# The 72 stores of the merge's tanh gates: issued from ScalarE's queue instead of SP's

## The chip, the cores and the metric

One core of one Trainium2 chip runs the kernel. The metric is the device time of one execution in microseconds (us), the median of several; lower is better. The core has five engines that run their own instruction queues in order: TensorE (PE, matmuls and transposes into PSUM), VectorE (DVE), ScalarE (ACT), GpSimd (POOL), and SP, which computes nothing and here issues all transfers between SBUF and DRAM.

## The reference, cut to what matters

Two layers of a mixer over 512 latent tokens and 256 context tokens, width 1024, all in float32. Each layer makes from `h @ w_in` the inputs of three attention branches (neighbourhood, latent, differential), twelve gate paths `z`, and three merge gates `gm` of 1024 channels each, 24 blocks of 128 channels. Only the end of a layer matters here:

```
y = (sigmoid(g_na)   * ((o_na   * silu(z_na))   @ w_br[0])
   + sigmoid(g_mla)  * ((o_mla  * silu(z_mla))  @ w_br[1])
   + sigmoid(g_diff) * ((o_diff * silu(z_diff)) @ w_br[2]))
x = x + gate * (y @ w_out)
```

The sigmoid is computed as (tanh(g/2) + 1) / 2. The tanh is what is stored and read again later.

## The kernel before, in words

A layer (`mixer`) has two parts. In the first, twelve steps each project the operands of one attention pair (`proj_nd`, `proj_m`), one gate path (`zgate`) and some of the 24 merge-gate blocks (`gm`), while the attention of the pair of the step before runs (`attn`). `NGM` says how many gate blocks fall to which step, `ADA` which steps also take a part of the modulation vector (`ada_half`). In the second part, `branch` multiplies the attention outputs with `w_br` and merges them with the stored gates, and `out_proj` does the last projection.

Every float32 matmul is three matmuls (`mm3`, lines 115 to 117) of operands that are split into a high and a low part. A weight block comes by DMA into one of seven raw buffers (`ws`, line 138), ScalarE makes the high part (`w`, line 122), VectorE or GpSimd the low part (line 127), in one of nine buffers each.

`gm` (line 1001 and after) takes one block of 128 gate channels: 24 matmuls for each range of tokens into the one PSUM bank `fl`, then ScalarE's tanh from `fl` into the one SBUF buffer `th` (line 1011), then a DMA of `th` to the DRAM tensor `thd` (line 1012). Layer 0 has two ranges of 384 tokens for a block, layer 1 one range of 512, so there are 24 x 2 + 24 = 72 tanhs and 72 stores, of 192 and 256 KB. `zgate`, `ada_half` and some of the second part use the same bank `fl`. In the second part line 987 reads the gates back, one load for each block and branch.

The order of each engine's queue is fixed when the kernel is built. A planner simulates the engines on a model of their costs; at each point it takes, of the instructions that could start, the one with the earliest due time. The due times are set with `at`: a base for the step, an offset for the kind of work (`PRI`) and some hand-set shifts (`SHIFT`). The planner also places the waits between engines. Other DMAs that the text speaks of: line 232 loads `aw`, the weights of `ada_half`, into two buffers for the matmuls of line 237; line 598 loads `ct` for the latent attention; line 974 loads `uraw`, the attention outputs. ScalarE's other work in the same stretches: the exponentials of the softmax (line 717), the copies of transposed probabilities out of PSUM (line 705), and the high parts of lines 122 and 522.

Of the kernel before, what the change touches and what calls it, by code (L numbers as in the profile page):

```python
# [52 lines left out]
class Mixer:  # L53
# [948 lines left out]
    def gm(self, l, i, pool):  # L1002
        nc = self.nc
        ws = self.units(self.io["w_gm"][l, i])
        for c0, w in self.cols(l):
            c = slice(c0, c0 + w)
            ps = self.fl()
            for k in range(KT):
                self.mm3(ps[:, :w], ws[k], [self.h[j][:, k, c] for j in range(2)], k == 0, k == KT - 1)
            th = pool.tile([P, 512], F32, tag="th", name=self.n("th"))[:, :w]  # L1010
            nc.scalar.activation(th, ps[:, :w], AF.Tanh, scale=0.5)
            nc.sync.dma_start(self.th[i][:, c], th)

    def diff_tables(self, l, pool):
        nc = self.nc
# [174 lines left out]
```

## Time and profile before

| | |
|---|---|
| median of 3 runs | 1928.85 us (1923.16 to 1929.49) |
| the profiled execution | 1923.38 us |
| its span, first to last instruction | 1921.6 us |
| PE busy | 1857.9 us, 97% of the span |
| VectorE busy | 1192.0 us, 62% |
| ScalarE busy | 938.8 us, 49% |
| GpSimd busy | 762.1 us, 40% |
| DMA | 1 queue for the program's data, 41.1% of 16 engines' span |

In the rows, PE is TensorE's matmuls, PEld its weight loads, and a name with q (SPq, ACTq) is an engine's sequencer, which waits and issues while the engine itself is idle. "A <- B" in a list of waits says that A stood idle until B ended. L1012 is line 1012 of the kernel.

### The profile page before, as it was taken

What the parts mean: (1) busy time and instruction counts of PE and PEld (TensorE: products, weight loads), DVE (VectorE), ACT (ScalarE), POOL (GpSimd) and SP (SyncE); (2) the same over time, 40 slices, a digit from 0 to 9 for tenths busy, and PEclk for the clock granted to TensorE, in tenths of its full rate; (3) what the DMA queues carried; (4) which work ended last, traced back from release to release, by engine and by line L of the source; (5) the groups of instructions that cost most, each with busy time, mean ns of one, the idle gap of its engine ahead of it and who ended that gap; (6) DMA issues with size and microseconds to landing.
All of it is one profiled execution on the core that took longest, in us unless ns stands there. A gap on an engine that the chain in (4) does not pass through costs nothing.

```text
span 1921.6 us, 33888 instructions
## 1 busy us (share of the span) xinstructions
PE 1857.9 (97%) x11707; PEld 1725.0 (90%) x11707; DVE 1192.0 (62%) x2698; ACT 938.8 (49%) x2422; POOL 762.1 (40%) x1057
## 2 busy tenths in 40 slices
PE   7999999999999999999999999999899999999998
PEld 3999999999899998999999988898799798889878
DVE  4556567646865655557663455668668665766763
ACT  4445455445644544546432344556456455555531
POOL 3343333233433333243355454444334343443363
PEclk8999999999999999999999999999999999999999
DMA  9454223343545334324655234423522523442663
GB/s 314 159 178 142 64 67 100 102 132 86 159 136 169 85 120 134 103 89 120 228 161 171 99 122 132 122 75 91 167 64 71 161 78 92 123 131 60 192 194 117
DMA packets 184824, 245.38 MB, mean 128 GB/s; under 512 B 22454, under 2 KB 148040, under 8 KB 184652
## 3 DMA queue, kind: packets, MB, share of 16 engines
q1 hardware_dynamic: 184652, 243.21, 41.1%
q8 instruction: 93, 1.52, 0.3%
q14 instruction: 79, 0.65, 0.1%
HBM read 190.45 MB, written 46.53 MB: 123 GB/s over the span
## 4 chain that ended last, share of the span: by engine, by line
PE 87%; DVE 4%; DMA 3%; ACT 2%; POOL 2%; issue 1%; SPq 0%; ACTq 0%; DVEq 0%; POOLq 0%
PE pj L115 11%; PE pj L117 11%; PE pj L116 11%; PE fl L115 10%; PE fl L116 10%; PE fl L117 9%; PE sc L712 6%; PE bk L867 4%; PE bk L702 4%; PE bk L833 2%; PE sc L754 1%; PE pj L662 1%; DMA aw<-in_w_ada 1%; PE pj L473 1%; PE fl L237 1%
## 5 line engine op out<-in xcount | busy, mean ns | idle before, releaser
L122 ACT CAST w<-ws 128x384 fp32r<-128x384 f32 (+3 forms) x520 | 237.4, 473 | 256.2 <-PE fl L116 153.0
L127 POOL TENSOR_TENSOR w<-ws,w 128x384 fp32r<-128x384 f32 (+3 forms) x260 | 242.5, 938 | 298.3 <-ACT w L122 275.3
L115 PE MATMUL fl<-h,w 128*128 128x384 f32 (+1 forms) x864 | 314.4, 364 | 6.4 <-DVE zs L414 4.7
L115 PE MATMUL pj<-w,h 128*128 128x384 f32 (+2 forms) x944 | 313.6, 335 | 2.0 <-DVE kl L127 1.1
L117 PE MATMUL fl<-h,w 128*128 128x384 f32 (+1 forms) x864 | 310.7, 360 | 2.2 <-DVE w L127 1.3
L116 PE MATMUL pj<-w,h 128*128 128x384 f32 (+2 forms) x944 | 309.8, 329 | 1.0 <-POOL w L127 1.0
L116 PE MATMUL fl<-h,w 128*128 128x384 f32 (+1 forms) x864 | 310.0, 359 | 0.0
L117 PE MATMUL pj<-w,h 128*128 128x384 f32 (+2 forms) x944 | 309.2, 331 | 0.7 <-POOL h L127 0.6
L127 DVE TENSOR_TENSOR w<-ws,w 128x384 fp32r<-128x384 f32 (+2 forms) x260 | 170.6, 659 | 72.4 <-ACT w L122 67.2
L167 POOL TENSOR_TENSOR ss<-ss,nhalf 128x4 f32<-128x4 f32 (+1 forms) x144 | 143.1, 994 | 177.8 <-DVE ss L166 161.7
L717 ACT ACTIVATE P<-sc,st 128x768 f32<-128x768 f32 (+1 forms) x192 | 159.5, 832 | 100.8 <-DVE st L798 43.0
L764 POOL TENSOR_SCALAR P<-P,st 128x512 f32<-128x512 f32 (+1 forms) x128 | 107.9, 845 | 241.1 <-DVE st L760 211.4
L115 PEld LDWEIGHTS pj<-w,h 128*128 128x128 f32 x944 | 178.5, 190 | 8.9 <-issue 3.0
L117 PEld LDWEIGHTS pj<-w,h 128*128 128x128 f32 x944 | 177.7, 189 | 5.7 <-DVE h L368 3.3
L115 PEld LDWEIGHTS fl<-h,w 128*128 128x128 f32 x864 | 163.1, 189 | 20.2 <-DVE zs L414 6.5
L116 PEld LDWEIGHTS pj<-w,h 128*128 128x128 f32 x944 | 179.1, 190 | 1.7 <-POOL w L127 1.3
L706 DVE TENSOR_TENSOR pt<-bk,pt 128x512 fp32r<-128x512 f32 (+1 forms) x256 | 147.5, 585 | 52.1 <-ACT pt L705 49.6
L117 PEld LDWEIGHTS fl<-h,w 128*128 128x128 f32 x864 | 162.9, 189 | 14.0 <-POOL w L127 1.6
L116 PEld LDWEIGHTS fl<-h,w 128*128 128x128 f32 x864 | 163.1, 189 | 9.5
L705 ACT CAST pt<-bk 128x512 fp32r<-128x512 f32 (+1 forms) x256 | 127.2, 507 | 77.0 <-PE bk L702 73.9
L712 PE MATMUL sc<-qk,qk 96*128 96x512 f32 (+3 forms) x592 | 144.3, 337 | 1.4 <-ACT P L717 1.0
L702 PE MATMUL bk<-cst,P 128*128 128x128 f32 x832 | 128.9, 273 | 5.0 <-DVE ss L166 2.0
(239 smaller groups left out, 3915.5 us busy)
## 6 DMA issues: line engine op xcount, KB each, us to landing
ws<-in_w_qkv SPq DMA_DIRECT2D x128, 192.0 KB
ws<-in_w_gm SPq DMA_DIRECT2D x96, 192.0 KB
aw<-in_w_ada SPq DMA_DIRECT2D x32, 512.0 KB
ct<-cqd SPq DMA_DIRECT2D x40, 384.0 KB
ct<-ckd SPq DMA_DIRECT2D x48, 256.0 KB
ws<-in_w_z SPq DMA_DIRECT2D x48, 192.0 KB
thd<-th SPq DMA_DIRECT2D x48, 192.0 KB
ws<-in_w_br SPq DMA_DIRECT2D x48, 192.0 KB
```

Source lines behind the costliest of these rows:

```text
L115: mm(out, a[0], b[0], start=first, stop=False)
L116: mm(out, a[0], b[1], start=False, stop=False)
L117: mm(out, a[1], b[0], start=False, stop=last)
L122: nc.scalar.copy(hi, src)
L127: (nc.gpsimd if le == "g" else nc.vector).tensor_tensor(lo, src, f(hi), ALU.subtract)
L167: nc.gpsimd.tensor_tensor(out, out, self.nhalf[:, :cols], ALU.pow)
L702: nc.tensor.transpose(pt[:, i * P:(i + 1) * P], src[:, (b0 + i) * P:(b0 + i + 1) * P], self.ident)
L705: nc.scalar.copy(h, v)
L706: nc.vector.tensor_tensor(lo, v, f(h), ALU.subtract)
L712: mm(s[:, d0:d0 + w], x, y, start=i == 0, stop=i == len(ops) - 1)
L717: nc.scalar.activation(p, src, AF.Exp, bias=st[:, m:m + 1], accum_out=st[:, o:o + 1])
L764: nc.gpsimd.tensor_scalar(p, p, st[:, 4 + m:5 + m], 0.0, ALU.mult, ALU.add)
```

## The change

The DMA of line 1012 is issued from ScalarE's queue. It moves the same bytes between the same places, and it still has to follow the tanh of line 1011. All other DMAs stay on SP's queue.

```diff
             th = pool.tile([P, 512], F32, tag="th", name=self.n("th"))[:, :w]
             nc.scalar.activation(th, ps[:, :w], AF.Tanh, scale=0.5)
-            nc.sync.dma_start(self.th[i][:, c], th)
+            nc.scalar.dma_start(self.th[i][:, c], th)
```

## Rows read from the trace of the kernel before

**Rows 1.** The page, busy time and share of the span and instructions, by engine.

```profile
PE 1857.9 (97%) x11707; PEld 1725.0 (90%) x11707; DVE 1192.0 (62%) x2698; ACT 938.8 (49%) x2422; POOL 762.1 (40%) x1057
```

**Rows 2.** Busy time by engine in the two stretches that hold the stores.

```profile
core 0: us, PE busy (x) PEld busy (x) DVE busy (x) ACT busy (x) POOL busy (x), PEclk, DMA share, GB/s
142.00:918.00 776.00, 762.78 (x5068) 732.50 (x5068) 487.29 (x1132) 402.10 (x1059) 266.31 (x382) 1.00 0.38 115
1196.00:1786.00 590.00, 573.04 (x3613) 517.41 (x3612) 397.36 (x929) 322.50 (x828) 242.35 (x347) 0.99 0.35 105
```

**Rows 3.** Waits of PE, whole span: us in total, times, longest.

```profile
PE fl L237 <- DMA aw<-in_w_ada: 6.2, 4, 3.1
...
PE bk L702 <- DVE pt L706: 1.4, 3, 0.8
...
PE fl L115 <- ACT th L1011: 1.2, 4, 0.4
...
PE sc L712 <- ACT P L717: 1.0, 2, 0.8
```

**Rows 4.** The page, chain that ended last, shares by engine.

```profile
PE 87%; DVE 4%; DMA 3%; ACT 2%; POOL 2%; issue 1%; SPq 0%; ACTq 0%; DVEq 0%; POOLq 0%
```

**Rows 5.** Instructions of the store's line and the tanh's line: ns min/median/max.

```profile
L1012 SPq DMA_DIRECT2D thd<-th x72: 319/327/1151, 142.6 to 1785.2; - x72
L1012 SPq EVENT_SEMAPHORE  x70: 17/17/17, 141.2 to 1785.1; - x70
...
L1011 ACT ACTIVATE th<-fl x72: 479/492/619, 142.1 to 1782.7; 128x384 f32<-128x384 f32 x48, 128x512 f32<-128x512 f32 x24
```

**Rows 6.** Waits of SP's queue: us in total, times, longest.

```profile
SPq L138 <- POOL w L127: 270.2, 150, 10.2
...
SPq L1012 <- ACT th L1011: 88.1, 41, 6.9
...
SPq L1012 <- ACT qk L122: 15.0, 7, 7.4
...
SPq L1012 <- ACT qk L130: 6.9, 2, 4.4
...
SPq L1012 <- ACT pt L705: 2.9, 6, 1.3
```

**Rows 7.** ScalarE in time around three tanhs: start us, us, instruction [idle before].

```profile
171.71 0.51 ACT L1011 ACTIVATE th<-fl 128x384 f32<-128x384 f32 x1
172.10 0.39 ACT L705 CAST pt<-bk 128x256 fp32r<-128x256 f32 x1
...
912.67 0.48 ACT L1011 ACTIVATE th<-fl 128x384 f32<-128x384 f32 x1
913.18 0.36 ACT L870 COPY ot<-bk 64x256 f32<-64x256 f32 x1
...
1782.68 0.59 ACT L1011 ACTIVATE th<-fl 128x512 f32<-128x512 f32 x1
1783.17 0.36 ACT L705 CAST pt<-bk 128x256 fp32r<-128x256 f32 x1
```

**Rows 8.** SP's issue of the store at 171.71, start us, us.

```profile
172.25 0.32 SPq L1012 DMA_DIRECT2D thd<-th  x1
```

**Rows 9.** ScalarE's longest wait by cause: us in total, times, longest.

```profile
ACT w L122 <- PE fl L116: 153.0, 152, 4.8
```

**Rows 10.** SP's issues in time before two late loads: start us, us, issue.

```profile
1365.90 0.33 SPq L1012 DMA_DIRECT2D thd<-th  x1
...
1368.02 0.33 SPq L598 DMA_DIRECT2D ct<-ckd  x1
1368.62 0.93 SPq L232 DMA_DIRECT2D aw<-in_w_ada  x2
...
1488.39 0.38 SPq L1012 DMA_DIRECT2D thd<-th  x1
1489.33 0.33 SPq L138 DMA_DIRECT2D ws<-in_w_gm  x1
1489.75 0.41 SPq L598 DMA_DIRECT2D ct<-ckd  x1
1490.25 0.93 SPq L232 DMA_DIRECT2D aw<-in_w_ada  x2
```

## The prediction

> **What bounds the kernel now.** I read the page first: PE is busy 1857.9 of 1921.6 us, 97% [rows 1]. Whatever moves the time has to add to PE's idle time, 63.7 us in all, or take from it. The busy time by stretch says how much of that lies where the stores are: 776.00 - 762.78 = 13.2 us from 142 to 918 us and 590.00 - 573.04 = 17.0 us from 1196 to 1786 us, together 30.2 us [rows 2]. That is the most that any rearrangement there could give back. The list of PE's waits then shows what this idle time is made of: many small waits, the largest group 6.2 us for the loads of `aw`, and almost none for ScalarE: 1.2 us for the tanh itself, 1.0 us for the exponentials [rows 3]. The chain of work that ended last agrees: PE 87%, DMA 3%, ACT 2%, and SP's own issuing 0% [rows 4].
>
> The store itself is next. On SP one issue takes 319 to 1151 ns, 327 in the median [rows 5]. SP often stands before it: 88.1 + 15.0 + 6.9 + 2.9 = 112.9 us in 41 + 7 + 2 + 6 = 56 waits ended by ScalarE [rows 6]. The reader should see that SP is early, not late: it waits for the tanh and issues at once, as at 172.25 us, 0.03 us after the tanh that began at 171.71 and took 0.51 [rows 7, 8].
>
> **Part 1: what SP is rid of.** 72 issues x 0.327 us = 23.5 us of issuing and the 112.9 us of standing. What stood behind a store can go earlier, in the longest case by 7.4 us [rows 6]. Most of that is weight loads, and they are not short: SP waits 270.2 us for their buffers to come free from GpSimd alone [rows 6], and ScalarE's high parts wait 153.0 us for PE to give buffers back [rows 9]. Loads that come earlier only fill raw buffers earlier. That is worth nothing as long as the seven raw buffers stay ahead; if that cover is gone, each late block is a PE wait on line 115 to 117, which now hardly occurs.
>
> The exception is `aw`, the only load for which PE loses time. Before the largest of its waits a store is issued at 1365.90, but a load of `ct` comes between, at 1368.02, and `aw` goes at 1368.62, 2.4 us after the store was done [rows 10]: it was not the store that held it. At 1488.39 a store took 0.38 us and two more loads followed it before `aw` at 1490.25 [rows 10]; without it `aw` goes about 0.4 us earlier. Bounds of the gain: 0 and the whole 6.2 us; I take 0.4, by the second place, where the store's own slot is all that `aw` gets back.
>
> The Trainium skill, "DMA: Bandwidth & Descriptors", section "Issuing engines are not separate DMA queues", says that issuing from several engines only saves the sequencer's time to start a transfer. By it SP's standing would count for nothing and the sum would gain at most the store's slot; by the list of SP's waits, read alone, a gain up to the 6.2 us would be open. The order of issues before the late loads sides with the page at both places.
>
> **Part 2: what ScalarE takes on.** The trace has no DMA issued by ScalarE, so the price comes from SP's rows. The issue must wait until the tanh is written (0.03 us on SP), then takes 0.327 us, and the next instruction can no longer start before the tanh has ended, as it does now at 172.10 against an end at 172.22, some 0.1 us [rows 7]. That is 0.46 us where ScalarE has work ready. It has in 27 of the 72 cases, the first at 171.71 and the last at 1782.68 [rows 7]: 27 x 0.46 = 12.4 us. In 17 more the gap is under 0.36 us, like the 0.03 us behind the tanh of 912.67 [rows 7], and 0.18 us is lost on average: 3.1 us. In the other 28 the idle time covers the issue. Sum: 15.5 us of delay on an engine that is idle 373.9 + 267.5 = 641 us in these stretches [rows 2]. Bounds: 0, if the order is such that no store meets ready work, and 72 x (0.03 + 1.151 + 0.1) = 92 us if each issue took SP's longest.
>
> How much reaches the end? ScalarE's share of the chain is 2% for 49% busy [rows 1, 4], so one us in 25 of its time counts: 15.5 / 25 = 0.6 us. The cover is the slack of PE behind ScalarE: VectorE's low parts come between, and PE waits for those of line 706 1.4 us in all [rows 3]. As one late copy also delays VectorE's instruction behind it, I double this to 1.3 us. What is late next, should the cover go, is the copy of line 705, then the low part of line 706 and PE's product with the values.
>
> Each store has besides a wait of its own ahead of it, which never lasted on SP: 17 ns, 70 times [rows 5]. What it is for the row doesn't say. I cost it at nothing; if it lasted on ScalarE, the exponentials would queue behind it.
>
> **Part 3: nothing from the buffer.** `th` has one buffer, but the store is already issued 0.03 us after most tanhs, so it can't come free sooner, and the transfer is the same.
>
> **Part 4: the order.** The planner builds all queues anew with the store on ScalarE, and may place other instructions elsewhere. No row prices that. Bounds: it gives back the 30.2 us of idle time in these stretches [rows 2], or adds as much. With no reason for a sign I take 0 and keep a part of both ends for the range.
>
> **Sum.** 1.3 - 0.4 = about +1 us: 1924.4 us against the profiled 1923.38 (span 1921.6 and 1.8 around it). The median of the runs, 1928.85, lies 5.5 us above that execution, so the forecast for a median is 1930 us. Differences under 0.3%, 5.8 us, can't be told from no change here.
>
> **Rivals.**
> Slower by ScalarE's queue: the store stops the softmax. Place: copies of line 705 and exponentials of line 717 right behind a store. Price: the 15.5 us in full, or 72 x 0.46 = 33 us if the new order sets each store ahead of ready work: 1944 to 1962 us. It decides when PE's slack behind ScalarE is under 0.46 us, or where the store's second wait lasts. For it: 27 back-to-back places. Against it: PE waits so little for ScalarE now [rows 3], and 641 us of idle time. Chance 0.2.
>
> Faster by SP's queue: freed loads end the 6.2 us of `aw` waits and some of the small ones: about 1921 us. For it: 112.9 us of standing. Against it: the order before those loads [rows 10], and this only just passes 0.3%. Chance 0.05.
>
> A new order that matters more than either: up to some 15 us both ways, half of the 30.2: 1914 to 1944 us. For it: PE's idle time is many waits of single places [rows 3], which any shift of the queues exchanges for others. Against it: the work per engine is the same. Chance 0.35: 0.2 faster, 0.15 slower by over 0.3%.
>
> The change doing nothing that can be seen is part of the forecast.
>
> **How the numbers follow.** Forecast, the order much as it is and both prices hidden: 0.40, its own range 1923 to 1934.6 us. Faster 0.2 + 0.05 = 0.25, slower 0.2 + 0.15 = 0.35. The range runs from 1914, the lower end of a new order, to 1950, inside ScalarE's rival; some 0.1 lies above and 0.05 below.
>
> **What would show it.** Right: no wait of SP on line 1012; 72 issues of some 0.33 us on ScalarE's queue with idle time of that size behind 40 or so tanhs; PE's busy time within 1 us of 1857.9 and its idle time within 5 us of 63.7; waits of PE for ScalarE of a few us. Wrong: waits of PE for lines 705, 706 or 717 of 10 us and more (ScalarE's rival); the `aw` waits gone and the time down (SP's rival); PE's waits at quite other places with as much work done (a new order). An issue on ScalarE far from 0.33 us would make part 2 wrong even if the time is right.

## The result, and the profile after

The changed kernel takes 1946.34 us (median of 4 runs, 1944.1 to 1948.49) against 1926.01 us for the kernel before (4 runs). The ratio is 1.0107, 95% interval 1.0078 to 1.0135: slower by some 20 us. The profiled execution took 1947.38 us, with a span of 1945.2 us, 23.6 us more than the span of before.

The page of the changed kernel, busy time by engine, which answers to [rows 1]:

```profile
PE 1868.8 (96%) x11707; PEld 1734.5 (89%) x11707; DVE 1199.0 (62%) x2698; ACT 938.2 (48%) x2422; POOL 766.7 (39%) x1057
```

The same instructions ran on every engine, and ScalarE's busy time is the old one to 0.6 us. PE shows where the time is, in two halves: its idle time went from 63.7 to 1945.2 - 1868.8 = 76.4 us, 12.7 us more, and its busy time, for the same 11707 matmuls, from 1857.9 to 1868.8 us, 10.9 us more. Together that is the 23.6 us. The split holds for this pair of executions: TensorE's mean granted clock (1 is full speed) differs between executions of one kernel, from 0.989 to 0.996 among 23 of the kernel before, which took 1928.9 and 1916.63 us at those two ends.

The store itself is what the change says. The instructions of line 1012 in the changed kernel (ns min/median/max, first and last start), which answer to [rows 5]:

```profile
L1012 ACTq DMA_DIRECT2D thd<-th x72: 325/326/365, 144.3 to 1805.8; - x72
L1012 ACTq EVENT_SEMAPHORE  x58: 17/17/17, 143.8 to 1733.4; - x58
```

72 issues of 0.326 us on ScalarE's queue, none over 0.365 us, and each wait that stands as an instruction of its own lasts 17 ns. The last store starts at 1805.8 us, where it started at 1785.2 before [rows 5]: 20.6 of the 23.6 us are lost by the time that the last gate is made. ScalarE in time at one of these stores, in the changed kernel:

```profile
173.18 0.51 ACT L1011 ACTIVATE th<-fl 128x384 f32<-128x384 f32 x1
173.56 0.39 ACT L705 CAST pt<-bk 128x256 fp32r<-128x256 f32 x1
173.72 0.33 ACTq L1012 DMA_DIRECT2D thd<-th  x1
174.09 0.28 ACT L632 ACTIVATE qn<-pj 128x128 f32<-128x128 f32 x1
```

The tanh ends at 173.69. Here the planner set a copy between tanh and store, and the issue runs from 173.72 to 174.05 while that copy still works until 173.95. In 33 of the 72 cases one to three other instructions stand between the two; in the other 39 the store follows its tanh directly.

The waits of PE in the changed kernel (total, times, longest), which answer to [rows 3]:

```profile
PE pj L473 <- DVE qn L467: 11.3, 8, 4.2
PE fl L237 <- DMA aw<-in_w_ada: 11.2, 4, 5.6
...
PE bk L845 <- POOL s L842: 2.7, 1, 2.7
...
PE sc L712 <- DMA qk<-qk: 2.0, 1, 2.0
```

The same list of the kernel before, for two lines that [rows 3] don't have:

```profile
PE pj L350 <- DVE ssx L166: 9.4, 1, 9.4
PE pj L473 <- DVE qn L467: 6.3, 5, 2.8
```

None of the changed kernel's four is a wait for ScalarE. (PE's longest single wait, over 9 us on line 350, stands at the start of both kernels and has no part in the difference.) The waits for VectorE's `qn` grew from 6.3 to 11.3 us and those for `aw` from 6.2 to 11.2 us, though SP now issues these loads with no store ahead of them. SP in time before the longest wait for `aw`, in the changed kernel, which answers to the first half of [rows 10]:

```profile
1376.39 0.33 SPq L598 DMA_DIRECT2D ct<-cqd  x1
1377.13 0.33 SPq L598 DMA_DIRECT2D ct<-ckd  x1
1377.73 0.93 SPq L232 DMA_DIRECT2D aw<-in_w_ada  x2
```

PE's product with them, before (the wait that [rows 10] lead up to) and after (start, duration, idle time before):

```profile
1375.48 1.08 PE L237 MATMUL fl<-aw,sT 128*32 128x256 f32 x8 [3.07 <-DMA aw<-in_w_ada]
```

```profile
1384.57 1.08 PE L237 MATMUL fl<-aw,sT 128*32 128x256 f32 x8 [5.58 <-DMA aw<-in_w_ada]
```

From issue to product it is 1375.48 - 1368.62 = 6.86 us before and 1384.57 - 1377.73 = 6.84 us after: the load is as fast as it was. But PE had other work for 6.86 - 3.07 = 3.8 us of that before, and for 6.84 - 5.58 = 1.3 us now. The order leaves it less to do in between.

The other half, PE's busy time, is seen in stretches around a wait. Busy time (instructions) of PE, PEld, DVE, ACT and POOL, then granted clock, DMA share and GB/s, in the changed kernel:

```profile
304.00:312.50 8.50, 8.50 (x64) 8.43 (x63) 7.83 (x21) 5.49 (x16) 6.82 (x7) 1.00 0.36 104
312.50:317.20 4.70, 0.51 (x5) 0.27 (x3) 4.51 (x10) 3.26 (x8) 2.25 (x4) 0.94 0.48 153
317.20:323.50 6.30, 6.10 (x21) 5.71 (x22) 4.19 (x11) 2.75 (x7) 1.36 (x2) 0.50 0.14 31
323.50:330.00 6.50, 6.50 (x54) 6.47 (x52) 3.71 (x7) 2.48 (x6) 0.00 (x0) 1.00 0.40 115
```

PE is busy throughout, then for 0.51 of 4.70 us, and behind that the granted clock is 0.50, the lower of its two levels (1.2 instead of 2.4 GHz): 6.10 us of work hold 21 matmuls, where the next 6.50 us hold 54 (not all of the same shape). The mean granted clock tells how much of this there is. Span and clock of the core before, and after:

```profile
core 0: 1921.6 us, clock 0.993
```

```profile
core 0: 1945.2 us, clock 0.984
```

With half the time lost at the lower level, that is from 0.007 x 1921.6 / 0.5 = 27 us (the start of the program included) to 0.016 x 1945.2 / 0.5 = 62 us, some 35 us more. One us of work at half clock is half a us too long, so 35 us explain up to 17 of PE's longer busy time; 10.9 were measured. Counted by the trace's clock records instead, PE worked 25.2 us at half clock before and 53.2 us after; half of the difference is 14.0 us. The seven stretches at half clock that lie in the two parts with the stores, in the changed kernel, each follow or overlap a PE wait of 1.6 to 5.6 us; but behind a wait of 2.8 us at 735.1 us in the kernel before the clock stayed at 1.00, so not every wait brings one.

### The profile page after: what moved, and what is told of

It reads as the page before. It is cut to its first block, busy times and chain, and to the rows that moved or that the text cites. A ratio compares the mean times of both kernels' runs of the same rounds, so it can differ in the third digit from the quotient of the medians.

```text
span 1945.2 us, 33846 instructions
## 1 busy us (share of the span) xinstructions
PE 1868.8 (96%) x11707; PEld 1734.5 (89%) x11707; DVE 1199.0 (62%) x2698; ACT 938.2 (48%) x2422; POOL 766.7 (39%) x1057
## 4 chain that ended last, share of the span: by engine, by line
PE 86%; DVE 5%; DMA 3%; ACT 2%; POOL 2%; issue 2%; SPq 0%; DVEq 0%; ACTq 0%; POOLq 0%
PE pj L115 11%; PE pj L117 11%; PE pj L116 11%; PE fl L115 10%; PE fl L116 10%; PE fl L117 10%; PE sc L712 6%; PE bk L867 4%; PE bk L702 4%; PE bk L833 2%; PE sc L754 1%; DMA aw<-in_w_ada 1%; PE pj L662 1%; PE pj L473 1%; PE fl L237 1%
## 5 line engine op out<-in xcount | busy, mean ns | idle before, releaser
L127 DVE TENSOR_TENSOR w<-ws,w 128x384 fp32r<-128x384 f32 (+2 forms) x260 | 175.5, 678 | 81.8 <-ACT w L122 74.5
```

Of the source, the lines that this page charges most:

```text
L127: (nc.gpsimd if le == "g" else nc.vector).tensor_tensor(lo, src, f(hi), ALU.subtract)
```

## The experiments

An engine's queue can be held to a given order with edges between neighbours that add no semaphore:

```diff
+        for a, b in zip(q, q[1:]):
+            tc.add_manual_dep(ins[b], ins[a].name, dep, reason="pin")
```

So the two things that the change does, another engine that issues and another order of the queues, can be taken apart. Between the kernels before and after, 4892 lines of PE's program stand elsewhere; in the traces, at least 1424 of the 11707 matmuls have to be moved to make one order of PE into the other.

**The order of before, stores on ScalarE.** All queues keep the order of before; the store stands right behind its tanh. The trace has the 11707 matmuls in the order of before, and ScalarE's instructions too.

```diff
-            nc.sync.dma_start(self.th[i][:, c], th)
+            nc.scalar.dma_start(self.th[i][:, c], th)
...
+            pin(nc, tc)
```

> All queues keep the order of the kernel before, instruction by instruction; only the 72 stores leave SP's queue and stand in ScalarE's right behind their tanh. So this holds the price of the issue on ScalarE and nothing of a new order. If the new order costs the 20 us (my theory): a ratio to the kernel before of 0.997 to 1.003, about 1926 us. If ScalarE's queue costs it (the rival): at least half of the loss, a ratio of 1.005 to 1.012, and more than in the changed kernel where 33 of its 72 stores stand two to four instructions behind the tanh, since here each stands directly behind it.

Measured: 1924.01 us (12 runs) against 1922.73 (23 runs), ratio 1.0003 (0.9988 to 1.0017). Its page, its stores and two of its waits of PE, and the first line of SP's waits:

```profile
PE 1859.7 (97%) x11707; PEld 1726.8 (90%) x11707; DVE 1194.8 (62%) x2698; ACT 939.4 (49%) x2422; POOL 761.7 (40%) x1057
```

```profile
L1012 ACTq DMA_DIRECT2D thd<-th x72: 325/326/365, 142.7 to 1786.4; - x72
```

```profile
...
PE fl L237 <- DMA aw<-in_w_ada: 7.9, 4, 3.0
PE pj L473 <- DVE qn L467: 6.3, 5, 2.8
```

```profile
SPq L138 <- POOL w L127: 306.6, 160, 10.5
```

ScalarE at the first of the places where it has work ready behind the tanh, which answers to [rows 7]:

```profile
171.67 0.51 ACT L1011 ACTIVATE th<-fl 128x384 f32<-128x384 f32 x1
172.22 0.33 ACTq L1012 DMA_DIRECT2D thd<-th  x1
172.58 0.37 ACT L705 CAST pt<-bk 128x256 fp32r<-128x256 f32 x1 [0.40 <-ACT th L1011]
```

The copy of line 705 now starts 0.40 us after the tanh has ended, where it started 0.12 us before that [rows 7]. Compared tanh by tanh between the two traces, the next instruction starts later by 18.8 us in all: 13.4 us in the 27 cases with work ready, 5.4 us in the 17 with a small gap, nothing in the other 28. So ScalarE is held up, but it costs PE nothing: PE's idle time is 1923.7 - 1859.7 = 64.0 us, against 63.7. Nor does SP's relief give anything: its wait for raw buffers rose from 270.2 us [rows 6] to 306.6, and the waits for `aw` did not shrink (7.9 against 6.2 us).

**The order of after, stores on SP.** The other half alone: the same edges, now with the changed kernel's order.

```diff
             nc.sync.dma_start(self.th[i][:, c], th)
...
+            pin(nc, tc)
```

> All queues have the order of the changed kernel, but the 72 stores are issued by SP, each at its place in the planner's overall order. So this holds the new order and no issue on ScalarE. If the new order costs the 20 us (my theory): a ratio to the kernel before of 1.008 to 1.013, about 1945 us. If ScalarE's queue costs it: 0.997 to 1.004.

Measured: 1942.47 us (5 runs), ratio 1.0103 (1.0078 to 1.0127), the loss of the changed kernel within its interval. Its waits of PE:

```profile
PE pj L473 <- DVE qn L467: 12.0, 8, 4.2
...
PE fl L237 <- DMA aw<-in_w_ada: 8.1, 2, 5.5
...
PE sc L712 <- DMA qk<-qk: 3.2, 1, 3.2
PE bk L845 <- POOL s L842: 2.7, 1, 2.7
```

These are the waits of the changed kernel, with no store on ScalarE's queue. Its page (the span is 1939.6 us, the mean granted clock 0.988):

```profile
PE 1863.3 (96%) x11707; PEld 1731.2 (89%) x11707; DVE 1200.1 (62%) x2698; ACT 937.4 (48%) x2422; POOL 765.9 (39%) x1057
```

PE's idle time is 1939.6 - 1863.3 = 76.3 us, that of the changed kernel (76.4). Its busy time is 5.4 us over that of before in this execution, at a higher clock than the 0.984 of the changed kernel's. The loss is the order.

**Another order with the stores on SP.** Is it any order but the one of before?

```diff
-    PRI = dict(step=2200, attn=500, prep=1000, pm=1500, ...
+    PRI = dict(step=2200, attn=500, prep=1000, pm=1520, ...
```

> The stores are SP's as before; one offset of a due time is 1520 instead of 1500 (the latent projection), which changes 1367 lines of PE's order against 4892 in the changed kernel. If any order other than the one of the kernel before is slower (theory: the due times are fitted to that one order): a ratio of 1.002 to 1.010. If orders drawn by chance scatter around the old one: 0.995 to 1.005 with either sign. If ScalarE's queue is all that matters: 0.998 to 1.002.

Measured: 1929.11 us (12 runs), 1.0033 (1.0018 to 1.0048), with 1367 of PE's lines elsewhere. Another order costs, but a third of the 1.07%.

**The longest waits filled.** The changed kernel's order, with PE's waiting matmuls set behind the work that follows them at seven of its long waits (4.2 us at 317.22, 5.6 at 1384.57, and five of 1.4 to 3.1). In PE's order, at the first of them (this is a list of instructions, not code):

```diff
 L702 bk<-cst,P
-L473 pj<-cst,qn   (waited 4.21 us)
 L702 bk<-cst,P
 L115 fl<-h,w
 ...
+L473 pj<-cst,qn
```

> The order of the changed kernel, stores on ScalarE, but at seven places where PE stood 1.4 to 5.6 us there (19.8 us in all: lines 473, 237, 473, 473, 712, 237, 237) the waiting matmuls are put behind the PE work that followed them, as much of it as the wait was long. If the loss sits in these waits and in the half clock behind them (my theory): at least half of the 20 us comes back, a ratio to the kernel before of 1.000 to 1.006. If the new order costs by many small shifts everywhere (the rival): less than a quarter comes back, 1.008 to 1.011.

Measured: 1950.39 us (4 runs) against 1922.72 (7 runs), 1.015 (1.013 to 1.017). Nothing came back, and neither forecast held. But the seven fills did not take PE's idle time away. The page (the span is 1952.8 us):

```profile
PE 1872.6 (96%) x11707; PEld 1740.2 (89%) x11707; DVE 1200.1 (61%) x2698; ACT 937.6 (48%) x2422; POOL 767.4 (39%) x1057
```

PE is idle for 1952.8 - 1872.6 = 80.2 us, against 76.4 in the changed kernel. The waits for `qn` of line 467 and for `aw` fell from 22.5 to 9.0 us together, and others came in their place. PE in time at the first of the seven, in this kernel:

```profile
310.86 0.60 PE L702 MATMUL bk<-cst,P 128*128 128x128 f32 x4
316.53 1.12 PE L702 MATMUL bk<-cst,P 128*128 128x128 f32 x4 [5.07 <-POOL P L764]
...
319.36 0.52 PE L115 MATMUL fl<-h,w 128*128 128x384 f32 x1
...
322.00 0.34 PE L116 MATMUL fl<-h,w 128*128 128x384 f32 x1
```

The matmul of line 473 is out of the way, and the next one in the queue waits 5.07 us for GpSimd in its place. Behind it a matmul of the same shape takes 0.52 us, and 2.6 us later 0.34: the granted clock is 0.50 from 316.50 to 320.80 us and 1.00 behind that. So filling one place moved the wait to another; whether the loss would go if the waits themselves went is not shown by this run.

**Four issues for one store, order of before.** How much does ScalarE's cover hold?

```diff
-            nc.scalar.dma_start(self.th[i][:, c], th)
+            for j in range(4):
+                nc.scalar.dma_start(self.th[i][:, c0 + j * w // 4:c0 + (j + 1) * w // 4], th[:, j * w // 4:(j + 1) * w // 4])
```

> The order of the kernel before; each store is issued by ScalarE right behind its tanh as four DMAs of a quarter each: 288 issues of some 0.33 us, 94 us of ScalarE's queue instead of 23.5. If ScalarE's idle time covers issues (theory): 1.000 to 1.004. If the single issue was only just covered, so that its cost starts here: 1.006 to 1.02. By the share of the chain that the prediction used, one us in 25 doubled, 94 us would give 7.5 us, 1.004.

Measured: 1947.44 us (4 runs), 1.0138 (1.0123 to 1.0153). Its stores (line 1013 there) with the first of those who waited for them (total, times), and its waits of PE:

```profile
L1013 ACTq DMA_DIRECT2D thd<-th x288: 326/444/2006, 142.7 to 1807.9; - x144
...
  ACT pt L705: 12.2, 5
  ACT qk L122: 10.0, 4
```

```profile
PE pj L662 <- POOL qn L657: 10.5, 6, 2.4
...
PE bk L702 <- DVE pt L706: 4.1, 3, 2.4
```

The theory of this run fell (1.000 to 1.004), and the 7.5 us by the share of the chain were 25 us. An issue in a row of four takes 0.444 us in the median and up to 2.006: the first of a row 0.326 in the median, the three behind it some 0.45. Now the copies of line 705 stand behind the stores and PE behind their low parts, 4.1 us where it was 1.4 [rows 3]. PE's wait on line 662 grew most, to 10.5 us in 6 places from 0.9 in one; it is for GpSimd, whose own waits for ScalarE's copy of line 639 grew from 82.2 to 107.2 us. So the mechanism of the rival "ScalarE's queue stops the softmax" exists; at one issue for a store it does not decide. Each of the four DMAs also moves a quarter (384 or 512 bytes for a partition instead of 1536 or 2048), and this run doesn't part the number of issues from the size of the pieces.

**Pairs: one set of due times, with the stores on SP and on ScalarE.** Seven kernels ask whether the planner's order is worse whenever it counts the issues on ScalarE, or was so once by chance. The due times are shifted by one value of `PRI`, or by a fixed draw for each place:

```diff
-        self.tc.cur_priority = self.base + o + i * self.PRI["step"] // 20
+        self.tc.cur_priority = self.base + o + i * self.PRI["step"] // 20 + jitter(self.where, key, i)
```

`pm` at 1520, stores on ScalarE:

> The changed kernel with one due time of 1520 instead of 1500 (the latent projection): another order drawn with the stores on ScalarE, 1933 lines of PE's order from the changed kernel's and 5531 from that of the kernel before. If orders far from the old one are slower (theory): 1.005 to 1.013. If the changed kernel's order was only a bad draw: about as likely under 1.003 as over.

`gm` at 2600 instead of 2500, stores on SP:

> The kernel before, stores on SP, with one due time of 2600 instead of 2500 (the merge gates): another order, 2010 lines of PE's order away. If the loss grows with the distance from the order that the due times were set for: 1.003 to 1.008. If the issue on ScalarE misleads the planner: 0.998 to 1.003, as SP's orders stay good.

Draw A (up to 100 either way), stores on SP:

> The kernel before, stores on SP, with every due time moved by a fixed draw between -100 and +100 (a step is 2200): an order 5364 lines of PE's queue away from the old one, further than the changed kernel's 4892. If the loss goes with the distance from the old order, whoever issues the stores (my theory now; so far 1367, 2010, 4892 and 5531 lines gave 1.0033, 1.0043, 1.0107 and 1.0134): 1.009 to 1.015. If a planner that counts the issue on ScalarE makes worse orders (the rival): 1.001 to 1.006, like the two other orders with stores on SP.

Draw B (up to 200 either way), stores on SP:

> As before it, with another draw between -200 and +200: 5766 lines away, stores on SP. Distance: 1.010 to 1.016. The planner's count of the issue on ScalarE: 1.001 to 1.007.

`attn` at 520 instead of 500, stores on ScalarE:

> The changed kernel, stores on ScalarE, with one due time of 520 instead of 500 (the attention): a third order drawn with the stores on ScalarE, 5469 lines from the old one. Distance: 1.009 to 1.015. The planner's count of the issue: 1.008 to 1.015 too, so this run alone tells nothing apart; it shows how far orders of one kind scatter, and with the two before it whether stores on ScalarE lie above stores on SP at the same distance.

Draw A and draw B, stores on ScalarE:

> The due times of the far order a (1.0079 with stores on SP), but with the stores on ScalarE as in the change. If the distance from the old order is all: close to 1.008, within 0.002 (the order is 6519 lines away instead of 5364). If an order that the planner draws with the issue on ScalarE is worse in itself: 1.011 or more.

> The due times of the far order b (1.0071 with stores on SP) with the stores on ScalarE, 7064 lines from the old order. Distance alone: 1.005 to 1.010. A planner misled by the issue on ScalarE: 1.011 or more, as in the run before it.

Measured, as ratios to the kernel before with their intervals, each with the number of PE's lines that stand elsewhere than before:

| due times | stores on SP | stores on ScalarE |
|---|---|---|
| as before | 1 | 1.0107 (1.0078 to 1.0135), 4892 lines |
| `pm` 1520 | 1.0033 (1.0018 to 1.0048), 1367 | 1.0134 (1.0115 to 1.0153), 5531 |
| `gm` 2600 | 1.0043 (1.0028 to 1.0057), 2010 | not run |
| `attn` 520 | not run | 1.0106 (1.0088 to 1.0125), 5469 |
| draw A | 1.0079 (1.0062 to 1.0096), 5364 | 1.0151 (1.0136 to 1.0166), 6519 |
| draw B | 1.0071 (1.0046 to 1.0095), 5766 | 1.0156 (1.0139 to 1.0173), 7064 |

By the medians, all five orders drawn with the stores on ScalarE are slower than all four new ones drawn with them on SP, and within each of the four pairs ScalarE costs 0.7 to 1.1%. But it also takes the order farther away, and distance has a price without it: with the stores on SP, 1367 and 2010 lines elsewhere cost 0.3 and 0.4%, over 5000 cost 0.8 and 0.7%. At like distance (4892 to 5766 lines) the orders drawn for SP lose 0.7 to 0.8% and those drawn for ScalarE 1.1 to 1.3%. Counted in the traces, as the least number of PE's matmuls to move, it comes out the same: 1424 for the changed kernel, 1473 and 1705 for the two draws on SP. So the larger part of the loss goes with being far from the order of before; that the rest belongs to ScalarE's orders is likely, but some of these intervals overlap. Of the two theories of these runs, neither holds alone: with the stores on SP, both draws lost less than distance asked (at least 1.009 and 1.010), and draw A more than the planner's count allowed (at most 1.006); with them on ScalarE, both lost more than distance alone allowed (at most 1.010).

The pages of draw A, stores on SP and on ScalarE:

```profile
span 1935.8 us, 33897 instructions
...
PE 1859.9 (96%) x11707; PEld 1729.1 (89%) x11707; DVE 1196.0 (62%) x2698; ACT 936.1 (48%) x2422; POOL 761.7 (39%) x1057
```

```profile
span 1947.4 us, 33841 instructions
...
PE 1870.5 (96%) x11707; PEld 1736.4 (89%) x11707; DVE 1196.1 (61%) x2698; ACT 937.1 (48%) x2422; POOL 764.8 (39%) x1057
```

An order far away brings the idle time of the changed kernel with the stores on SP too (1935.8 - 1859.9 = 75.9 us; 76.9 with them on ScalarE). Between these two it is PE's busy time that differs, by 10.6 us, and with it the granted clock: 0.992 and 0.985. Part of that is the execution and not the order, as the profiled one of draw A on SP (1937.65 us) is the fastest of its four, and the others (1940.66 to 1941.38 us) had 0.988 and 0.989.

No version beat the kernel before; the one with the stores on ScalarE in the old order equals it.

## Why the prediction was right or wrong

The time fell inside the range (1914 to 1950), but not by the likeliest case: 1930 us with the order much as it was, against 1946.34. That it lies inside is luck. The upper end was there for ScalarE's rival, which the runs exclude; the range of a new order, which was the cause, ended at 1944 us.

**What bounds the kernel: one reading was wrong.** The `aw` loads, at 6.2 us, are not the largest group of PE's waits. Line 350 waits 9.4 us, once, at the start, and line 473 waits 6.3 us for VectorE. The first changes nothing; the second is a group that the new order made longer, by 5.0 us, and no term of the sum looked at it.

**Part 1, SP: right.** A gain of 0.4 us was taken. With the order held, SP only waits longer for buffers, and the loads of `aw` are as late as before. The page of the Trainium skill that was cited, "DMA: Bandwidth & Descriptors", section "Issuing engines are not separate DMA queues", says that issuing from several engines only saves the sequencer's time to start a transfer. This case agrees: SP was rid of 72 issues, and the time did not change (1.0003).

**Part 2, ScalarE: right.** The issue was priced at 0.327 us from SP's rows and takes 0.326. The second wait, costed at nothing, takes 17 ns. The delay on ScalarE was put at 15.5 us and is 18.8 us with the order held, as the 17 small gaps lose 0.32 us on average and not 0.18. It was to reach the end as 1.3 us; parts 1 to 3 together were to add 1 us, and a ratio of 1.0003 is 0.6 us of 1922.73, with an interval of -2.3 to 3.3. The factor of one us in 25, doubled, is not borne out by that: the interval holds nothing as well, and at four issues it gave 7.5 us where 25 were measured. That each issue must follow the end of the tanh held. With the store right behind the tanh it kept the next instruction back in all 72 cases; in the changed kernel it did not, as the planner set other work between in 33.

**Part 3, the buffer: nothing was expected,** and the old order with the stores on ScalarE leaves room for 2 or 3 us at most, if no other part hides it.

**Part 4, the order: this step failed.** It said "With no reason for a sign I take 0". The order cost 1942.47 - 1922.73 = 19.7 us with the stores on SP, the whole loss. The bound, 30.2 us, contained it, though not for its reason. Two things were wrong in taking 0. First, the order of before is not one of many equals: four other orders with the stores on SP all lost, 0.3 to 0.8%. Its due times carry hand-set shifts; that these are why every draw away from them lost is argued, not shown. The measurement shows the sign, and the prediction had given a better order 0.2 and a worse one 0.15. Second, the size: the rival of a new order went to 15 us, half of PE's idle time in the two stretches, as if idle time were all that an order can change. In the profiled execution idle time rose by 12.7 us; the other 10.9 us are PE's own work made longer, by the lower clock behind its waits as far as the clock records tell, for which the sum had no term.

**The rivals.** ScalarE's queue gave a time (1944 to 1962 us) that fits, for a wrong reason: what was to show it, waits of PE for lines 705, 706 or 717 of 10 us and more, is absent (1.1, 0.7 and 0.6 us are the largest), and the old order with the stores on ScalarE excludes it. SP's queue did not turn faster. The new order was the right rival; what was to show it, PE's waits at other places with as much work done, is in the profile after.

**What stays open.** Why the planner, once it counts an issue on ScalarE, lands so far from the order of before, and whether its orders are worse than others as far away, is not settled: the pairs give 0.7 to 1.1% with the distance in it, some 0.3 to 0.6% without, and no kernel took the planner's count apart. Nor was the issue itself taken out of the other orders drawn for it; in the changed kernel's it costs nothing that can be seen (1.0107 with it, 1.0103 without). Filling seven waits did not repair the order, but neither did it make PE's idle time smaller.

## What to carry to other kernels

Where a planner builds the queues, a one-line change of the issuing engine is two changes: hold the order and move the instruction, then hold the instruction and move the order, and measure both. Here the first cost nothing and the second 1%. In a kernel whose due times were set by hand, price a new order as a loss: all nine new orders of the planner lost here, 0.3 to 1.6%. And price PE's waits at more than their length, since work behind them can run at half clock.

## What was unexpected of the hardware

A DMA issue on ScalarE's queue can run beside ScalarE's own instruction before it, as at 173.72 us. The instruction behind it waits, 0.40 us at 172.58 with the old order, but here that delay, 18.8 us in all, cost the kernel nothing. The kernel with four in a row lost 1.4%: they take 0.444 us each in the median, up to 2.006 us, against 0.326 and 0.365 singly. And the waits of 4.2 and 5.6 us on PE had stretches at the lower clock with them (0.50 from 317.20 to 323.50 us and from 1381.60 to 1388.40 us). In the profiled execution PE's work took 10.9 us longer, nearly as much as its idle time grew, 12.7 us.
